# Rotary queries computed with channels on partitions: two heads per product, tables turned once, and one transpose group of the up stage issued nine products later

## The chip, the cores and the metric

The kernel runs on one NeuronCore of one Trainium2 chip. The metric is the device time of one execution in microseconds (us); the time of a kernel is the median of its runs. Five engines work side by side, each through its own queue in order: TensorE (PE, matrix products, with a separate row PEld for loading weights), VectorE (DVE), ScalarE (ACT), GpSimd (POOL) and SyncE (SP, which issues the DMAs). They wait for each other by semaphores. Products land in PSUM, which has eight banks of 128 x 512 floats.

## The reference, cut to what matters

One layer of a streaming encoder on 512 tokens of width 1024, in float32. The first sub-layer has three parallel token mixers (pooling, latent attention, spatial gating), merged by gates; the second is a gated MLP with a short convolution. The change is in the attention's rotary queries (and, for one group of transposes, at the start of the MLP):

```python
def _apply_rope(x, cos, sin):
    x1, x2 = jnp.split(x, 2, axis=-1)                 # 32 + 32 channels
    return jnp.concatenate([x1 * cos - x2 * sin, x2 * cos + x1 * sin], axis=-1)

q = jnp.einsum('bsr,rhd->bshd', _rms_norm(cq, g_q), w_uq)      # 8 heads, 128 + 64 channels
q_nope, q_rope = q[..., :128], q[..., 128:]
q_rope = _apply_rope(q_rope, cos[:, :, None, :], sin[:, :, None, :])
k_rope = _apply_rope(kr, cos, sin)                             # one rotary key for all heads
s = einsum('bqhd,bkhd->bhqk', q_nope, k_nope) + einsum('bqhd,bkd->bhqk', q_rope, k_rope)
p = softmax(mask(s * 192 ** -0.5)); o = einsum('bhqk,bkhd->bqhd', p, v)
```

cos and sin depend on the token and on one of 32 frequencies, not on the head.

## The kernel before

Nearly every product is made from float32 operands that are split in a rounded high part and a low remainder (`...h`, `...l`); a product is then three matmuls, high by low, low by high and high by high (`mm3`, lines 106 to 108; `mm_chunk`, lines 113, 114 and 116, which is 24 matmuls of 512 columns over the eight 128-row pieces of the contraction). The split is one ScalarE cast (line 92 or 120) and one VectorE subtraction (line 93 or 121).

The program begins with the latent stage: products with eight pieces of the normalised input leave 448 latent channels for each of four token tiles in four PSUM banks (`lat`), tokens on partitions. ScalarE squares them (`sq`), POOL makes the norms (`rr`), ScalarE scales them (`cn`, lines 601 and 602). TensorE meanwhile computes gate blocks: `gate(b, m)` is one `mm_chunk` of 24 matmuls into a bank `pg`, and a Tanh on ScalarE (line 404). Twelve transposes (line 619, `ptc`) turn the normalised latents to channels on partitions, giving `cT0`, `cT1` (queries) and `cT2` (keys and values); nine more (`ptk`) turn the rotary key.

Rotary queries before: `rotary_queries` multiplies each token tile's latents by all 512 rotary channels (24 matmuls for four tiles, bank `pq`, tokens on partitions), multiplies the result on VectorE by tables `cosQ` and `sinQ` with the frequencies along the free axis (lines 661), combines halves on POOL (lines 669 and 672), splits into high and low on ScalarE and VectorE (lines 679 and 680), and leaves tiles `qst` in which a head has 64 high and 64 low channels side by side. `rotary_transposes(h)` then turns a head's four token tiles with four TensorE transposes (line 690, `ptq`) and one copy to `qrT`. Heads 0 to 3 are turned before the head loop, head h + 4 in the loop of head h.

The head loop: `scores(h)` (banks `sc`), `attend(h - 1)` (`po`), `project(h + 1)` (`pqn`), one gate block, `transposes(h)` (`ptp`, the probabilities turned, split to `PTh`, `PTl`). `scores(h)` needs `qrT[h]`. The bank that a `sc`, `pg` or `po` gets is the one that another tile has just given up, so a reader on ScalarE or VectorE that is late holds up TensorE.

The up stage (first products of the MLP) starts on the first two token tiles (columns 0 to 255) while the last two are still being normalised: `up_early(ms, half)` computes one half of the columns of output blocks `pzu`. `turn(tp, jp)` transposes two token tiles of the second normalisation `xr` (four transposes, `pth`), and `second_modulation` makes `h2T` out of it. `turn(1, 0)` is the first group that needs the last token tile.

The order on each engine is set when the program is built, by a scheduler that places instructions by its own estimate of time; `tc.issue_after` fixes single orders by hand. On the chip each engine then takes its queue strictly in that order.

## Time and profile before

| | before |
|---|---|
| time, median of 3 runs | 960.9 us (960.22 to 961.87) |
| the profiled execution's own time | 961.97 us |
| its span, first to last instruction | 960.2 us |
| granted TensorE clock, mean | 0.998 |
| PE busy | 946.6 us, 99% of the span |
| DVE, ACT, POOL busy | 579.6, 380.7, 285.1 us |
| HBM read | 116.83 MB, 124 GB/s over the span |

A profile is one execution. In a row of the timeline the first number is the start in us from the span's beginning, the second the length of the row (with its fellows, where "x8" says that eight follow each other), then engine, line, operation, output<-inputs, sizes; in brackets stands how long the engine was idle before, and what it waited for. Instructions of one engine overlap: the next one starts before the one ahead has ended, so the step from start to start is less than the length. In a row of the windows each engine has its busy time and count in that stretch, and then stand the granted clock (1.00 is full) and the DMA's share and rate.

### The profile page before, as it was taken

The numbers are of one execution on the slowest core, as the hardware profiler recorded it, in microseconds if no ns is written. First come the engines' busy times: TensorE is split into PE (matmuls) and PEld (weight loads), VectorE is DVE, ScalarE is ACT, GpSimd is POOL, SyncE is SP. The second block draws the span as 40 slices with busy tenths as digits, with TensorE's granted clock in tenths as the row PEclk, the third lists the DMA queues.
The fourth block names the chain that finished last, engine by engine and source line by source line (L and its number), as shares of the span: only waits on it lengthen the run. The fifth ranks groups of instructions, "written<-read, shape, count | busy, mean of one in ns | idle before, by whom it ended". The sixth has DMA issues, their size and how long they took to land.

```text
span 960.2 us, 12180 instructions
## 1 busy us (share of the span) xinstructions
PE 946.6 (99%) x4591; PEld 800.6 (83%) x4591; DVE 579.6 (60%) x841; ACT 380.7 (40%) x622; POOL 285.1 (30%) x257
## 2 busy tenths in 40 slices
PE   7999999999999999999999999999999999999996
PEld 6988888888888888888888889988888888888885
DVE  6968556456686566477333489576565564733368
ACT  4575556543333322233332345554444444322121
POOL 3752110122350023202112713021111121756653
PEclk9999999999999999999999999999999999999999
DMA  9812122045435633554343450134334433333222
GB/s 343 297 56 84 63 61 82 24 134 155 150 100 204 199 123 89 172 195 148 114 127 110 146 184 23 48 128 119 123 112 135 128 113 106 123 104 104 88 88 88
DMA packets 46139, 119.72 MB, mean 125 GB/s; under 512 B 5504, under 2 KB 8960, under 8 KB 46080
## 3 DMA queue, kind: packets, MB, share of 16 engines
q1 hardware_dynamic: 45648, 118.39, 38.1%
q8 instruction: 36, 0.59, 0.2%
q10 hardware_dynamic: 432, 0.55, 0.2%
q14 instruction: 23, 0.19, 0.1%
HBM read 116.83 MB, written 2.10 MB: 124 GB/s over the span
## 4 chain that ended last, share of the span: by engine, by line
PE 90%; DVE 4%; POOL 2%; DMA 1%; ACT 1%; issue 1%; POOLq 0%; SPq 0%; DVEq 0%; ACTq 0%
PE pzu L113 7%; PE pzu L114 7%; PE pzu L116 7%; PE pg L113 4%; PE pg L114 4%; PE pg L116 4%; PE py L113 4%; PE py L114 4%; PE py L116 4%; PE pyd L1149 3%; PE pyd L1152 3%; PE pyd L1151 3%; PE lat L531 2%; PE pu L113 2%; PE pu L114 2%; PE pa L113 2%
## 5 line engine op out<-in xcount | busy, mean ns | idle before, releaser
L93 DVE TENSOR_TENSOR wupl<-wup,wuph 128x1024 fp32r<-128x1024 f32 x38 | 48.2, 1270 | 71.8 <-PE pzu L116 45.8
L1118 POOL TENSOR_TENSOR d<-d,gtfb 128x512 f32<-128x512 f32 x44 | 73.4, 1690 | 37.8 <-DMA d<-in_wdn 37.2
L1421 POOL TENSOR_TENSOR zc<-zc 128x512 f32<-128x512 f32 x22 | 29.6, 1347 | 173.5 <-ACT zc L1420 131.4
L1123 DVE TENSOR_TENSOR dl<-d,dh 128x1024 fp32r<-128x1024 f32 x18 | 29.3, 1627 | 55.0 <-PE pyd L1149 50.2
L92 ACT CAST wuph<-wup 128x1024 fp32r<-128x1024 f32 x38 | 39.9, 1051 | 47.1 <-PE pzu L114 47.1
L422 POOL TENSOR_TENSOR mg<-mg,th 128x512 f32<-128x512 f32 x16 | 31.3, 1959 | 86.5 <-DVE th L419 86.5
L93 DVE TENSOR_TENSOR wgl<-wg,wgh 128x1024 fp32r<-128x1024 f32 x22 | 29.0, 1320 | 42.5 <-PE pg L116 21.6
L92 ACT CAST wbh<-wb 128x1024 fp32r<-128x1024 f32 x24 | 25.3, 1054 | 74.0 <-PE py L114 55.3
L872 DVE SCALAR_TENSOR_TENSOR ada<-adar,cact,ada 128x512 f32<-128x512 f32 x56 | 49.1, 906 | 0.5 <-DMA adar<-in_ada 0.5
L787 POOL TENSOR_SCALAR pe<-pe,mx 128x128 f32<-128x128 f32 (+3 forms) x32 | 17.0, 537 | 94.0 <-DVE mx L786 47.9
L1122 ACT CAST dh<-d 128x1024 fp32r<-128x1024 f32 x18 | 19.0, 1054 | 62.5 <-PE pyd L1152 42.0
L1403 ACT ACTIVATE zc<-pzu,cols 128x512 f32<-128x512 f32 x44 | 34.2, 780 | 22.3 <-PE pzu L116 17.8
L93 DVE TENSOR_TENSOR wbl<-wb,wbh 128x1024 fp32r<-128x1024 f32 x24 | 30.3, 1262 | 14.9 <-ACT wbh L92 6.5
L1406 DVE SCALAR_TENSOR_TENSOR zc<-pzu,cols,zc 128x511 f32<-128x511 f32 x44 | 32.6, 743 | 4.0 <-ACT zc L1403 4.0
L92 ACT CAST wgh<-wg 128x1024 fp32r<-128x1024 f32 x22 | 23.2, 1054 | 26.6 <-PE pg L114 22.1
L1410 DVE SCALAR_TENSOR_TENSOR zc<-pzu,cols,zc 128x510 f32<-128x510 f32 x44 | 32.6, 745 | 0.8
L419 DVE SCALAR_TENSOR_TENSOR th<-th,py 128x512 f32<-128x512 f32 x16 | 11.0, 687 | 35.6 <-PE py L116 35.6
L1420 ACT ACTIVATE zc<-zc 128x512 f32<-128x512 f32 x22 | 13.9, 631 | 40.5 <-DVE zc L1410 40.4
L925 POOL TENSOR_TENSOR asum<-apad 128x527 f32<-128x527 f32 x8 | 12.3, 1543 | 54.6 <-ACT apad L920 28.0
L300 DVE SCALAR_TENSOR_TENSOR acc<-ada,cact,acc 128x256 f32<-128x256 f32 (+1 forms) x29 | 26.2, 903 | 1.0
L1097 POOL TENSOR_TENSOR oraw<-oraw,gttb 128x512 f32<-128x512 f32 x6 | 10.5, 1778 | 47.2 <-DMA oraw<-in_wo 47.2
L1118 POOL TENSOR_TENSOR o<-o,gttb 128x512 f32<-128x512 f32 x10 | 17.1, 1736 | 12.8 <-DMA o<-in_wo 10.0
(1478 smaller groups left out, 3095.8 us busy)
## 6 DMA issues: line engine op xcount, KB each, us to landing
wup<-in_wup SPq DMA_DIRECT2D x44, 512.0 KB, 3.6
adar<-in_ada SPq DMA_DIRECT2D x64, 256.0 KB, 3.9
wb<-in_wb SPq DMA_DIRECT2D x24, 512.0 KB, 3.6
wg<-in_wg SPq DMA_DIRECT2D x22, 512.0 KB, 3.6
d<-in_wdn SPq DMA_DIRECT2D x22, 512.0 KB, 3.5
ada<-in_ada1p SPq DMA_DIRECT2D x24, 256.0 KB, 5.1
wa<-in_wa SPq DMA_DIRECT2D x8, 512.0 KB, 3.6
wsg<-in_wsg SPq DMA_DIRECT2D x8, 512.0 KB, 3.5
```

The costliest lines, as they stand in the source:

```text
L92: nc.scalar.copy(out=hi[:, :n], in_=raw[:, :n])
L93: ins = nc.vector.tensor_tensor(out=lo[:, :n], in0=raw[:, :n], in1=f(hi[:, :n]), op=ALU.subtract)
L113: nc.tensor.matmul(o, wh[:, c], xl[k], start=k == 0, stop=False)
L114: nc.tensor.matmul(o, wh[:, c], xh[k], start=False, stop=False)
L116: nc.tensor.matmul(o, wl[:, c], xh[k], start=False, stop=k == KT - 1)
L422: nc.gpsimd.tensor_tensor(out=merged[m], in0=merged[m], in1=th, op=ALU.add)
L872: nc.vector.scalar_tensor_tensor(out=acc[n], in0=src, scalar=cact[:, k : k + 1], in1=acc[n], op0=ALU.mult, op1=ALU.add,)
L1118: nc.gpsimd.tensor_tensor(out=halves[n], in0=halves[n], in1=gt[n], op=ALU.mult)
L1403: nc.scalar.activation(t, pz, AF.Identity, bias=cols[:, cc + 3 : cc + 4], scale=cols[:, cc + 2 : cc + 3])
L1406: nc.vector.scalar_tensor_tensor(out=t[:, 1:512], in0=pz[:, 0:511], scalar=cols[:, cc + 1 : cc + 2], in1=t[:, 1:512], op0=ALU.mult, op1=AL ...
L1410: nc.vector.scalar_tensor_tensor(out=t[:, 2:512], in0=pz[:, 0:510], scalar=cols[:, cc : cc + 1], in1=t[:, 2:512], op0=ALU.mult, op1=ALU.add,)
L1421: nc.gpsimd.tensor_tensor(out=val, in0=val, in1=gate, op=ALU.mult)
```

## The change

Rotary queries are now made with channels on partitions and tokens along the free axis: `rotary(p)` computes the 128 rotary channels of heads 2p and 2p + 1 for all 512 tokens (six matmuls into `pq`), so nothing is left to transpose for a head. The tables must then have frequencies on partitions: ScalarE writes `cosRx` and `sinRx` with each table repeated four times with its sign and the scale (line 614 after), eight transposes turn them between gate blocks 2 and 3 (`ptr`, line 623), two ScalarE copies take them out of PSUM. A rotation is one VectorE product with the cosines and four on 32 partitions each, which read the partner channels' partitions for the sines (line 686), one POOL addition, and per head a ScalarE cast and a VectorE subtraction on 64 partitions. Since an odd head's high part is on the upper partitions, the low rotary key `krL` is now doubled instead of filled with zeros. The split of the rotary weights moves behind the key's transposes (`rotary_weights`, two casts of 512). In the loop, `rotary` follows `project` in heads 0, 2 and 4. In the up stage the first three of eight steps of block 5 are issued ahead of `turn(1, 0)`.

```diff
-        nc.scalar.activation(cosQ, cosT, AF.Copy, scale=SCALE)
-        nc.scalar.activation(sinQ, sinT, AF.Copy, scale=SCALE)
...
-    nc.gpsimd.tensor_tensor(out=krl, in0=ro, in1=kr[:, :, 0:64], op=ALU.subtract)
+    nc.gpsimd.tensor_tensor(out=krl[:, :, 0:64], in0=ro, in1=kr[:, :, 0:64], op=ALU.subtract)
+    nc.gpsimd.tensor_copy(out=krl[:, :, 64:128], in_=krl[:, :, 0:64])
...
-    for m in range(2, 4):
-        th0.append(gate(0, m))
+    turns = []
+    wide = []
+    for nm, src, signs in (("cosR", cosT, (1.0, 1.0)), ("sinR", sinT, (-1.0, 1.0))):
+        wide.append(act_t(nm + "x", F32))
+        for g, sign in enumerate(signs):
+            nc.scalar.activation(
+                wide[-1].rearrange("p (t a b f) -> p t a b f", a=2, b=2, f=32)[:, :, :, g, :],
+                src.rearrange("p t (a f) -> p t a f", a=1).broadcast_to([P, TT, 2, 32]),
+                AF.Copy, scale=sign * SCALE,
+            )
+    th0.append(gate(0, 2))
+    for nm, src in zip(("cosR", "sinR"), wide):
+        pt = ps("ptr")
+        for t in range(TT):
+            nc.tensor.transpose(pt[:, t * P : (t + 1) * P], src[:, t * P : (t + 1) * P], ident)
+        table = act_t(nm, F32)
+        nc.scalar.copy(out=table, in_=pt)
+        turns.append(table)
+    th0.append(gate(0, 3))
...
-    def rotary_queries():
-        wh, wl = wsplit(A["wqr"], D, "wqr")
-        for t in range(TT):
-            pq = ps("pq")
...
-    def rotary_transposes(h):
-        pt = ps("ptq")
...
+    def rotary_weights():
+        raw = load(A["wqr"], D, "wqr")
+        for k in range(2):
+            wh = act_t(f"wqr{k}h")
+            wl = act_t(f"wqr{k}l")
+            c = slice(k * 512, (k + 1) * 512)
+            nc.scalar.copy(out=wh, in_=raw[:, c])
+            nc.vector.tensor_tensor(out=wl, in0=raw[:, c], in1=f(wh), op=ALU.subtract)
+            wqr.append((wh, wl))
...
+    def rotary(p):
+        pq = ps("pq")
+        c = slice(p * P, (p + 1) * P)
+        for k in range(2):
+            wh, wl = wqr[k]
+            mm3(pq, wh[:, c], wl[:, c], cT_hi[k], cT_lo[k], k == 0, k == 1)
+        tA = pt_t("qtA")
+        tB = pt_t("qtB")
+        nc.vector.tensor_tensor(out=tA, in0=pq, in1=turns[0], op=ALU.mult)
+        for j in range(4):
+            o = slice(32 * j, 32 * j + 32)
+            i = slice(32 * (j ^ 1), 32 * (j ^ 1) + 32)
+            nc.vector.tensor_tensor(out=tB[o, :], in0=pq[i, :], in1=turns[1][o, :], op=ALU.mult)
+        nc.gpsimd.tensor_tensor(out=tA, in0=tA, in1=tB, op=ALU.add)
+        for h in range(2):
+            q = act_t(f"qrT{2 * p + h}")
+            hi = slice(64 * h, 64 * h + 64)
+            lo = slice(64 - 64 * h, 128 - 64 * h)
+            nc.scalar.copy(out=q[hi, :], in_=tA[hi, :])
+            nc.vector.tensor_tensor(out=q[lo, :], in0=tA[hi, :], in1=f(q[hi, :]), op=ALU.subtract)
+            qrT.append(q)
...
     attention_weights(0)
-    rotary_queries()
+    rotary_weights()
+    rotary(0)
     th0.append(gate(0, 4))
     project(0)
     values(0, (0, 1))
-    rotary_transposes(0)
     th0.append(gate(0, 5))
...
-        if h + 4 < H:
-            rotary_transposes(h + 4)
         if h + 1 < H:
             project(h + 1)
+        if h in (0, 2, 4):
+            rotary(h // 2 + 1)
...
-    with tc.issue_after(up_early((4,), 0)):
+    up_early((4,), 0)
+    with tc.issue_after(up_early((5,), 0, range(3))):
         ins = turn(1, 0)
     with tc.issue_after(ins):
-        up_early((5,), 0)
+        up_early((5,), 0, range(3, KT))
```

What the scheduler makes of it is not seen in the diff. First place: TensorE between gate blocks 2 and 3 (`wgh`, `wgl` are the gate weights' high and low parts, `hT` the input's pieces). Before:

```order
L116 MATMUL pg<-hT6h,wgl 128x512
L116 MATMUL pg<-hT7h,wgl 128x512
L113 MATMUL pg<-hT0l,wgh 128x512
L114 MATMUL pg<-hT0h,wgh 128x512
L113 MATMUL pg<-hT1l,wgh 128x512
```

And TensorE there after:

```order
L116 MATMUL pg<-hT6h,wgl 128x512
L116 MATMUL pg<-hT7h,wgl 128x512
L623 MATMUL ptr<-ident,cosRx 128x128 x4
L623 MATMUL ptr<-ident,sinRx 128x128 x4
L113 MATMUL pg<-hT0l,wgh 128x512
L114 MATMUL pg<-hT0h,wgh 128x512
```

The two table turns stand at the head of block 3, and what they read comes from ScalarE. The same stretch of ScalarE's queue, before:

```order
L601 ACTIVATE cn_748<-lat_191,rr 128x256
L92 CAST wqrh<-wqr 128x1024
L602 ACTIVATE cn_745<-lat_190,rr 128x128
L602 ACTIVATE cn_748<-lat_191,rr 128x128
L404 ACTIVATE th_790<-pg 128x512
L92 CAST wgh<-wg 128x1024
L404 ACTIVATE th_823<-pg 128x512
```

And after:

```order
L597 ACTIVATE cn_744<-lat_189,rr 128x256
L92 CAST wgh<-wg 128x1024
L598 ACTIVATE cn_741<-lat_188,rr 128x128
L598 ACTIVATE cn_744<-lat_189,rr 128x128
L614 ACTIVATE cosRx<-cosT 128x8x32 x2
L614 ACTIVATE sinRx<-sinT 128x8x32 x2
L400 ACTIVATE th_793<-pg 128x512
L625 COPY cosR<-ptr 128x512
L625 COPY sinR<-ptr 128x512
L92 CAST wvh<-wv 128x512
L400 ACTIVATE th_840<-pg 128x512
```

The split of gate 4's weights took the place of that of the rotary weights, and the four table copies stand behind the last `cn` and ahead of gate 2's Tanh.

Second place: the end of the key's transposes on TensorE (`pwm` is head 0's combined query weight). Before, the rotary product follows with weights that were split long ago:

```order
L635 MATMUL ptk<-ident,kr 128x128 x4
L638 MATMUL ptk<-ident,krf 128x128
L642 MATMUL ptk<-ident,krl 64x128 x4
L737 MATMUL pwm<-wqk_872 128x128 x2
L106 MATMUL pq<-wqrl,cT0h 128x512
L107 MATMUL pq<-wqrh,cT0l 128x512
```

TensorE there after:

```order
L649 MATMUL ptk<-ident,kr 128x128 x4
L652 MATMUL ptk<-ident,krf 128x128
L656 MATMUL ptk<-ident,krl 128x128 x4
L733 MATMUL pwm<-wqk_888 128x128 x2
L106 MATMUL pq<-cT0l,wqr0h 128x512
L113 MATMUL pg<-hT0l,wgh 128x512
L114 MATMUL pg<-hT0h,wgh 128x512
```

And ScalarE after, at that place (before, `wqk0h` is followed by `wvh`):

```order
L123 ACTIVATE cT2h<-ptc,cols 128x512
L650 CAST krT<-ptk 128x512
L642 ACTIVATE kF<-ptc,cols 128x128
L120 CAST wqk0h<-pwm 128x256
L668 CAST wqr0h<-wqr 128x512
L668 CAST wqr1h<-wqr 128x512
```

One matmul of the rotary product now stands ahead of gate block 4, and its weights are split right there. Third place: TensorE in the up stage, where block 4's products end (`upl` and `uph` are the up weights' parts). Before:

```order
L108 MATMUL pzu<-h2T7h,uph_5109 128x256
L1267 MATMUL pth<-ident,xr_5330 128x128
L1267 MATMUL pth<-ident,xr_5367 128x128
L1267 MATMUL pth<-ident,xr_5330 128x128
L1267 MATMUL pth<-ident,xr_5367 128x128
L106 MATMUL pzu<-h2T0l,uph_5336 128x256
```

And TensorE there after:

```order
L106 MATMUL pzu<-h2T0l,uph_5304 128x256
L107 MATMUL pzu<-h2T0h,upl_5306 128x256
L108 MATMUL pzu<-h2T0h,uph_5304 128x256
L106 MATMUL pzu<-h2T1l,uph_5304 128x256
L107 MATMUL pzu<-h2T1h,upl_5306 128x256
L108 MATMUL pzu<-h2T1h,uph_5304 128x256
L106 MATMUL pzu<-h2T2l,uph_5304 128x256
L107 MATMUL pzu<-h2T2h,upl_5306 128x256
L108 MATMUL pzu<-h2T2h,uph_5304 128x256
L1260 MATMUL pth<-ident,xr_5298 128x128 x2
L1260 MATMUL pth<-ident,xr_5335 128x128
L1260 MATMUL pth<-ident,xr_5298 128x128
```

Nine products of block 5 moved ahead of the group.

## The prediction

> **What bounds the kernel now.** I read the page first, then the windows, then each engine's timeline around the three places of the change.

> ```profile
> PE 946.6 (99%) x4591; PEld 800.6 (83%) x4591; DVE 579.6 (60%) x841; ACT 380.7 (40%) x622; POOL 285.1 (30%) x257
> ```

> ```profile
> 110.00:200.00 90.00, 90.00 (x501) 78.73 (x500) 46.98 (x127) 48.43 (x120) 14.95 (x29) 1.00 0.18 57
> 600.00:610.00 10.00, 9.25 (x78) 9.02 (x78) 4.14 (x10) 5.38 (x10) 1.67 (x3) 1.00 0.18 54
> ```

> TensorE is busy for 946.6 of 960.2 us (the first row), and its busy time fills the head loop's window to the last hundredth, at the full clock (the 1.00 behind the five engines). Of the windows around the change only 600 to 610 has a hole, of 0.75. So the time moves by two things alone: matmul time taken out of TensorE's queue, and every moment in which that queue waits. DVE (47 of 90 us in the head loop) and ACT matter only where TensorE's next instruction waits for them.

> **Transposes taken out.** 32 query transposes go (8 heads x 4), 8 table transposes come. The price is in a row of eight:

> ```profile
> 94.20 1.03 PE L690 MATMUL ptq<-ident,qst 128*128 128x128 f32 x8
> 95.07 0.61 PE L737 MATMUL pwm<-wqk 128*128 128x128 f32 x4
> ```

> Eight take 95.07 - 94.20 = 0.87 us, 0.109 each, so 24 fewer are -2.62. The rotary product keeps its 24 matmuls of 512 columns, only with the operands' roles exchanged. The low key's four transposes go from 64 to 128 columns in: the rows of both forms are equally long (0.60 for four, below), so nothing.

> **The table turns, between gates 2 and 3.** They wait for ACT, which is late there:

> ```profile
> 57.10 0.31 ACT L240 ACTIVATE sinQ<-sinT 128x128 f32<-128x128 f32 x1
> 57.31 0.30 ACT L239 ACTIVATE cosQ<-cosT 128x128 f32<-128x128 f32 x1
> 58.18 0.39 ACT L586 ACTIVATE sq<-lat 128x256 f32<-128x256 f32 x1 [0.58 <-PE lat L531]
> 64.46 1.16 ACT L92 CAST wqrh<-wqr 128x1024 fp32r<-128x1024 f32 x1
> 65.40 0.76 ACT L602 ACTIVATE cn<-lat,rr 128x128 f32<-128x128 f32 x2
> 65.91 0.73 ACT L404 ACTIVATE th<-pg 128x512 f32<-128x512 f32 x1
> 79.06 0.71 ACT L679 CAST qst<-qro 128x256 fp32r<-128x256 f32 x2
> 64.52 0.39 PE L113 MATMUL pg<-hT0l,wgh 128*128 128x512 f32 x1
> ```

> The removed `sinQ` and `cosQ` lay ahead of an idle 0.58 us of ACT, so taking them out brings ACT no earlier to the later rows. From 58.18 to 65.91 it works without a break, and after the change on work of the same sizes: gate 4's split takes the place of the rotary weights' (both a cast of 128x1024). So the first table copy starts at 65.91. No row shows this copy (256 elements per partition, written in runs of 32); nearest is the cast of 128x256 from SBUF, 0.71 for two, next start after 0.31. The cosine table is done at 65.91 + 0.71 = 66.62, the sine table at 65.91 + 3 x 0.31 + 0.40 = 67.24. TensorE has finished gate 2 at 64.52. It turns the cosines from 66.67 (0.05 for the semaphore, an estimate: further down `kF` starts at 73.73, 0.03 after `cT2l` has ended at 72.95 + 0.75), the sines from 67.29, and begins gate 3 at 67.73. With 0.87 of work it would be 65.39: **+2.34 of waiting**, and since TensorE takes its queue in order, gate 3 waits with the turns, though its weights are there. Bounds: with the step of `sinQ` (0.21, length 0.30) 1.95; with that of the `cn` copies of 128x256 (0.36, length 0.56) 2.65. I take the middle, since its size and source are the same.

> **The rotary weights' split, ahead of gate 4.** After gate 3 TensorE turns latents and key and comes to the first rotary matmul, which now waits for `wqr0h` at the end of an ACT chain:

> ```profile
> 68.15 0.27 PE L619 MATMUL ptc<-ident,cn 128*128 128x128 f32 x1
> 70.11 1.36 PE L619 MATMUL ptc<-ident,cn 128*128 128x128 f32 x11
> 71.31 0.60 PE L635 MATMUL ptk<-ident,kr 128*128 128x128 f32 x4
> 71.86 0.60 PE L642 MATMUL ptk<-ident,krl 128*64 128x128 f32 x4
> 72.66 0.48 PE L106 MATMUL pq<-wqrl,cT0h 128*128 128x512 f32 x1
> 72.22 0.69 ACT L123 ACTIVATE cT2h<-ptc,cols 128x512 fp32r<-128x512 f32 x1
> 72.95 0.75 DVE L124 SCALAR_TENSOR_TENSOR cT2l<-ptc,cols,cT2h 128x512 fp32r<-128x512 f32 x1
> 73.73 0.37 ACT L628 ACTIVATE kF<-ptc,cols 128x128 f32<-128x128 f32 x1 [0.34 <-DVE cT2l L124]
> 74.00 0.36 ACT L120 CAST wqk0h<-pwm 128x256 fp32r<-128x256 f32 x1
> 78.46 0.62 ACT L92 CAST wvh<-wv 128x512 fp32r<-128x512 f32 x1 [4.09 <-issue]
> ```

> Let T be the end of gate 3 (70.11 before, when it had begun at 64.52: less the one transpose 5.48 for 24 matmuls, 0.228 each; after 67.73 + 5.48 = 73.21). TensorE reaches the rotary product at T + 2.55 before, at T + 2.66 after (the transpose of 68.15, which stood inside the block, now stands behind it). On ACT `wqk0h` starts at T + 3.89, with that one transpose T + 4.00; its path (`cT2h`, DVE's `cT2l`, `kF`) is unchanged. `wqr0h` follows 0.26 later (0.36 less the overlap that rows show) and takes 0.62, the row of a 128x512 cast: done at T + 4.88, TensorE goes on at T + 4.93 = 78.14. **+2.27 of waiting**. Before, this split lay at 64.46, when nobody needed it. Bounds: a cast as short as the one of 128x256 (0.40) gives 2.05, one as long as a whole 128x1024 (1.16) 2.8; the row of the same size decides. Behind the waiting matmul stands gate 4, whose weights were split at 64.46: it could run and doesn't. The weights' buffer is free later too: on SP's queue the load of gate 5's weights, and behind it those of gate 6 and of head 1, move from 67 to about 79.4, when DVE has made `wqr1l`. Gate 5 comes at 87.7, 8 us later, so that is hidden. POOL loses a memset and gains a copy of the low key, in the 8.93 us that the row of its first rotary step shows as idle.

> **DVE, POOL and the head loop.** A pair of heads costs DVE five products from PSUM, POOL one addition of 128x512, ACT two casts, DVE two subtractions:

> ```profile
> 77.35 0.68 DVE L661 TENSOR_TENSOR qtA<-pq,cosQ 128x512 f32<-128x512 f32 x1
> 77.95 0.68 DVE L661 TENSOR_TENSOR qtB<-pq,sinQ 128x512 f32<-128x512 f32 x1
> 77.58 0.74 POOL L669 TENSOR_TENSOR qro<-qtA,qtB 128x256 f32<-128x256 f32 x1 [8.93 <-DVE qtB L661]
> 80.37 1.19 POOL L669 TENSOR_TENSOR qro<-qtA,qtB 128x256 f32<-128x256 f32 x1
> 102.45 0.39 PE L108 MATMUL pqn<-cT1h,wqk1h 128*128 128x512 f32 x1
> 103.51 0.69 DVE L754 SCALAR_TENSOR_TENSOR q1l<-pqn,q1h 128x512 fp32r<-128x512 f32 x1 [2.52 <-ACT q1h L753]
> 106.95 0.61 PE L737 MATMUL pwm<-wqk 128*128 128x128 f32 x4
> 107.25 1.15 DVE L121 TENSOR_TENSOR PTl<-ptp,PTh 128x512 fp32r<-128x512 f32 x2
> 109.32 0.40 PE L774 MATMUL sc<-cT2l,q1h 128*128 128x512 f32 x1
> ```

> A product is 0.60 from start to start; I price those on 32 partitions the same, since they have the same 512 elements per partition. The first pair: TensorE ends its product at 78.14 + 26 x 0.228 = 84.1 (gate 4 in between), DVE's five end at about 87.3, POOL's addition at 89.1, ACT's casts at 90.2, DVE's subtractions at 91. Behind the casts ACT holds gate 4's Tanh, `q0h` and `V00h`, behind the subtractions DVE holds `q0l` and `V00l`. The scores come after 3 + 12 + 24 + 6 more matmuls and `pwm`, at 94.6: 3.5 us of cover, and Tanh and `q0h` take 1.1 of it. The tight spot is in head 0: counted from the end P of the projection (102.84 before), `q1l` ends at P + 1.36, five products add 3.0, gate weights 1.14, `PTl` 0.6: P + 6.1. The last score group of head 1 needs the bank that `PTl` then gives up; TensorE is there after 14 gate matmuls (3.2), 10 transposes (1.1) and the earlier scores (109.32 - 106.95 = 2.4), at P + 6.5. So it fits, by 0.3 to 0.4. ACT has the two casts in its queue until POOL's addition is done, and behind them the splits of `PTh` and of head 2's weights and head 1's first exponential, which TensorE needs at P + 8.8 to 9.0; the addition is 2 x 0.74 = 1.5 alone, 2 x 1.19 = 2.4 beside a DVE subtraction. With 1.8 it holds by about 0.2, with 2.4 TensorE waits 0.5. I take **+0.1**, bounds 0 and 0.6. In heads 2 and 4 the projection or the whole gate block lies between, 2 us more cover.

> **The up stage.** The four transposes waited for the last row tile; nine products now go first:

> ```profile
> 602.24 0.27 PE L1267 MATMUL pth<-ident,xr 128*128 128x128 f32 x1
> 603.26 0.55 PE L1267 MATMUL pth<-ident,xr 128*128 128x128 f32 x3 [0.75 <-ACT xr L1254]
> 603.56 0.36 PE L106 MATMUL pzu<-h2T0l,uph 128*128 128x256 f32 x1
> 602.39 1.52 ACT L1254 ACTIVATE xr<-x,rs 128x512 f32<-128x512 f32 x2 [7.29 <-POOL rs L145]
> 605.37 0.41 DVE L1297 TENSOR_TENSOR h2T0l<-h2f,h2T0h 128x256 fp32r<-128x256 f32 x1
> 606.94 0.28 PE L106 MATMUL pzu<-h2T0l,uph 128*128 128x256 f32 x1
> ```

> The step 602.24 to 603.26 is 0.91 longer than a transpose. Nine products of 0.12 (603.56 to 606.94 holds 24 of them and four transposes) are 1.08, so the group starts at 603.32 and does not wait. Next late is `h2T0l`: 605.78 before, some 0.2 later after, while its reader comes at 606.0 instead of 606.94. It just meets. **-0.82**, bounds -0.5 and -0.91.

> **Sum.** -2.62 + 2.34 + 2.27 + 0.1 - 0.82 = +1.27. The profiled execution had a span of 960.2 and a time of 961.97, 1.1 above the median of 960.9; its span would be 961.5, its time 963.2, the median **962.2**. All lower ends together give +0.5, all upper ones +2.9: 961.4 to 963.8. With 0.2% (1.9 us), about what a measurement of this kernel can tell from no change, that is mostly no change.

> **Rivals.** First, the turns and weights are in time and only the savings count: 960.9 - 3.4 = 957.5, or 959.9 if one of the two waits is there. For it speaks that ACT is busy for only 40% of the span; against it, that both places lie in a stretch where ACT's chain is the later one, by rows. Second, slower: products that read one group of 32 partitions and write another are slow. No row shows one. If each took twice 0.68, a pair would hold DVE 2.7 longer, and in head 0 `PTl` would come 2.4 behind TensorE: 964.6. It decides from about 0.25 per product, where the sum passes 1.9. Third, the clock. The two new holes are each over 2 us:

> ```profile
> 952.00:954.00 2.00, 0.81 (x7) 0.60 (x6) 1.93 (x6) 0.00 (x0) 0.85 (x1) 1.00 0.48 186
> 956.00:958.00 2.00, 0.00 (x0) 0.00 (x0) 1.04 (x2) 0.51 (x1) 0.96 (x1) 0.72 0.24 93
> ```

> The last matmul ends at 952.8, and the mean 0.72 says that the clock halved at 956.9, 4.1 us later. A hole of 2.3 us, or of 0.91 at 602, is shorter. If it did, with 4.1 us at half speed, each would cost 2.0: 966.2. [...]

> **Chances.** Forecast 0.69 (a fifth of it beyond +1.9), one wait absent 0.07, both absent 0.05, slow products 0.13, clock 0.04, something unseen 0.02. Faster by over 0.2%: 0.06. Within: 0.55 + 0.07 = 0.62. Slower: 0.14 + 0.13 + 0.04 + 0.01 = 0.32. The range leaves out both-absent, part of one-absent and the clock: 960.3 to 964.6.

> **What would show it.** Right: PE idle about 2.1 before `ptr` cosRx and 0.2 before sinRx, released by ACT; 2.3 before the first `pq`, released by ACT's rotary weights; no wait at `pth`; no new wait in the head loop above 0.5. Wrong: `ptr` or `pq` without idle time, DVE's sine products longer than 0.7, a clock under 1.00 after the holes, or a wait of `sc` for `PTl`.

## The result and the profile after

The changed kernel takes 966.3 us (median of 4 runs, 965.77 to 966.79) where the kernel before takes 961.1 beside it: a ratio of 1.0053, interval 1.0041 to 1.0065. It is slower by some 5 us, outside the range of the prediction. The profiled execution took 966.0 us with a span of 964.3, 4.1 more than the 960.2 of before. First the line of the page on the engines, then windows of the changed kernel (columns as in the prediction: length, then busy time of PE, PEld, DVE, ACT, POOL, then the granted clock, the DMA share and GB/s).

```profile
PE 946.4 (98%) x4567; PEld 799.1 (83%) x4567; DVE 586.9 (61%) x850; ACT 380.8 (39%) x623; POOL 284.2 (29%) x253
```

```profile
64.97:68.38 3.41, 1.75 (x11) 1.47 (x12) 1.23 (x1) 3.41 (x10) 3.31 (x7) 1.00 0.42 96
75.21:78.62 3.41, 1.38 (x11) 1.15 (x10) 3.10 (x6) 3.00 (x7) 0.00 (x0) 1.00 0.63 206
78.62:82.04 3.42, 3.42 (x10) 2.64 (x9) 0.80 (x2) 0.00 (x0) 0.00 (x0) 0.50 0.41 126
82.04:85.45 3.41, 3.41 (x16) 2.80 (x16) 0.00 (x0) 1.05 (x1) 0.00 (x0) 1.00 0.07 28
600.00:610.00 10.00, 10.00 (x87) 10.00 (x86) 5.90 (x12) 2.62 (x5) 2.72 (x5) 1.00 0.18 54
```

TensorE issues 24 matmuls fewer (4567 against 4591), yet its busy time fell by 0.2 us only, and not by 2.6. The largest part of the difference is in the window from 78.62 on: for 3.42 us the clock is 0.50, and 10 matmuls fill a window that holds some 16 at the full clock. Ahead of it lie two stretches with TensorE partly idle (1.75 and 1.38 busy of 3.41). At 600 to 610 the hole of 0.75 us is gone. The timeline of TensorE at the two holes and in the second head:

```profile
63.70 0.39 PE L116 MATMUL pg<-hT7h,wgl 128*128 128x512 f32 x1
66.63 0.66 PE L623 MATMUL ptr<-ident,cosRx 128*128 128x128 f32 x4 [2.54 <-ACT cosRx L614]
67.24 0.65 PE L623 MATMUL ptr<-ident,sinRx 128*128 128x128 f32 x4
75.52 0.61 PE L733 MATMUL pwm<-wqk 128*128 128x128 f32 x4
78.15 0.50 PE L106 MATMUL pq<-cT0l,wqr0h 128*128 128x512 f32 x1 [2.03 <-ACT wqr0h L668]
79.21 0.63 PE L113 MATMUL pg<-hT1l,wgh 128*128 128x512 f32 x1
104.53 0.39 PE L108 MATMUL pqn<-cT1h,wqk1h 128*128 128x512 f32 x1
111.70 0.50 PE L770 MATMUL sc<-cT2l,q1h 128*128 128x512 f32 x1 [0.15 <-DVE PTl L121]
114.58 0.51 PE L106 MATMUL pqn<-cT0l,wqk2h 128*128 128x512 f32 x1 [0.25 <-ACT wqk2h L120]
```

Both holes are where the prediction had them, released by the ScalarE instructions that it named. From start to start, less what a matmul (0.227) or transpose (0.109) takes, they cost 2.7 (66.63 - 63.70) and 2.2 us. The matmul at 79.21 is the sign of the half clock: the steps from there to 82.04 are 0.427 instead of 0.227, 1.7 us in all. In the second head TensorE waits for `PTl`, `wqk2h` and an exponential (which holds a bank): its steps are 0.31, 0.41 and 0.25 us longer there than normal, and the first steps behind them another 0.2 together, 1.2 us in all. The row at 104.53 is the last matmul of the projection ahead of them; the text comes back to it. The engines behind these waits:

```profile
65.73 0.85 ACT L614 ACTIVATE cosRx<-cosT 128x256 f32<-128x256 f32 x2
66.34 0.85 ACT L614 ACTIVATE sinRx<-sinT 128x256 f32<-128x256 f32 x2
77.47 0.63 ACT L668 CAST wqr0h<-wqr 128x512 fp32r<-128x512 f32 x1
106.88 2.79 DVE L686 TENSOR_TENSOR qtB<-pq,sinR 32x512 f32<-32x512 f32 x4
109.70 1.22 DVE L93 TENSOR_TENSOR wgl<-wg,wgh 128x1024 fp32r<-128x1024 f32 x1
109.82 2.26 POOL L687 TENSOR_TENSOR qtA<-qtA,qtB 128x512 f32<-128x512 f32 x1 [5.61 <-DVE qtB L686]
112.11 1.26 ACT L692 CAST qrT<-qtA 64x512 fp32r<-64x512 f32 x2 [2.58 <-POOL qtA L687]
```

What waits in the second head has two candidates: DVE's queue (five products, then a weight subtraction ahead of `PTl`), or POOL's addition, behind which ACT's queue stands.

### The profile page after: what moved, and what is told of

Read it like the earlier page. It is cut to its first block, busy times and chain, and to the rows that moved or that the text cites. A ratio compares the mean times of both kernels' runs of the same rounds, so it can differ in the third digit from the quotient of the medians.

```text
span 964.3 us, 12139 instructions
## 1 busy us (share of the span) xinstructions
PE 946.4 (98%) x4567; PEld 799.1 (83%) x4567; DVE 586.9 (61%) x850; ACT 380.8 (39%) x623; POOL 284.2 (29%) x253
## 4 chain that ended last, share of the span: by engine, by line
PE 90%; DVE 1%; POOL 0%; issue 0%; ACT 0%; POOLq 0%
PE pzu L114 7%; PE pzu L113 7%; PE pzu L116 7%; PE py L113 5%; PE py L114 5%; PE py L116 5%; PE pg L113 4%; PE pg L114 4%; PE pg L116 4%; PE pyd L1144 3%; PE pyd L1145 3%; PE pyd L1142 3%; PE pu L113 2%; PE pu L114 2%; PE pa L113 2%; PE pu L987 2%
## 5 line engine op out<-in xcount | busy, mean ns | idle before, releaser
L92 ACT CAST wuph<-wup 128x1024 fp32r<-128x1024 f32 x38 | 39.9, 1050 | 46.2 <-PE pzu L114 46.2
L92 ACT CAST wbh<-wb 128x1024 fp32r<-128x1024 f32 x24 | 25.3, 1054 | 73.5 <-PE py L114 55.3
L92 ACT CAST wgh<-wg 128x1024 fp32r<-128x1024 f32 x22 | 23.3, 1060 | 29.8 <-PE pg L114 19.8
```

The source lines that it names most:

```text
L92: nc.scalar.copy(out=hi[:, :n], in_=raw[:, :n])
```

## The experiments

All times are medians, all ratios are to the kernel before, run on the same chip (960.6 to 961.0). The theories carry the same letters throughout: A, the holes cost their length, and the clock halves wherever TensorE is idle for most of one window of 3.41 us (the length of the half clock in the profile above); B, it takes both holes; C, a wait taken away comes back elsewhere. D, P and V come with the experiments that they belong to; V and P are about the second head, V with DVE's queue as the cause and P with POOL's addition.

**The turns behind gate 3** (the first hole taken away):

```diff
     th0.append(gate(0, 2))
+    th0.append(gate(0, 3))
     for nm, src in zip(("cosR", "sinR"), wide):
 ...
         turns.append(table)
-    th0.append(gate(0, 3))
```

> The turns of the two tables stand behind gate 3 instead of between gates 2 and 3; all else as in the changed kernel. Theory A (each hole of TensorE costs its own length, and the clock is halved whenever TensorE is idle for more than about half of one of the 3.41 us windows that the clock's edges keep to, so that the second hole alone can do it): the first hole (2.8 us in the changed kernel) is gone, the second stays at 2.0 to 2.3 us because ScalarE's conversion of the rotary weights stands behind that of pwm; time 966.3 - 2.8 = about 963.5, and the half clock is still there in executions where the second hole lies well inside a window. Theory B (it takes both holes, the clock remembers the first): the half clock is gone as well, 966.3 - 2.8 - 1.7 = 961.8. Theory C (the hole only hides a lateness of ScalarE, which comes back at the next place): the second hole grows by what the first loses, up to 5 us, and the time stays within 0.5 us of 966.3.

961.8 us (11 runs, 960.61 to 963.67), ratio 1.0013 (1.0004 to 1.0021). The hole of the profiled execution and its windows:

```profile
75.15 0.50 PE L106 MATMUL pq<-cT0l,wqr0h 128*128 128x512 f32 x1 [2.02 <-ACT wqr0h L668]
```

```profile
71.57:74.98 3.41, 1.56 (x15) 1.37 (x12) 3.12 (x5) 3.06 (x8) 0.00 (x0) 1.00 0.59 197
74.98:78.40 3.42, 3.25 (x14) 2.73 (x15) 1.36 (x3) 0.64 (x2) 0.00 (x0) 1.00 0.26 59
```

The first hole is gone and the second stays as long as it was (2.02 against 2.03), so C falls. The median is the number of B (961.8) and not that of A (963.5), but the single runs say more. In this execution no half clock follows (1.00 in both windows). TensorE was busy for 1.56 of the 3.41 us of the first window, which hold most of the hole, against 1.38 in the changed kernel; where these 3.41 us begin is the author's estimate, since the clock has no edge there. The 11 runs fall in two groups with nothing between 961.95 and 963.22: seven with a mean clock of 0.997 to 0.998, mean time 961.20, and four with 0.995 to 0.996, mean 963.43. One hole of 2.02 us is thus followed by the half clock in some executions and not in others. That it was so in those four is inferred from their clock and time, since the profile is of one of the seven.

**The rotary weights converted ahead of gate 2** (the second hole taken away):

```diff
+    rotary_weights()
     th0.append(gate(0, 2))
 ...
     attention_weights(0)
-    rotary_weights()
     rotary(0)
```

> The rotary weights are converted ahead of gate 2, so that the first matmul of the rotary queries finds them; the turns stay between gates 2 and 3. Theory A: the second hole (2.0 to 2.2 us) and the half clock that lay behind it (1.7 us) go, the first hole stays, perhaps longer, since two ScalarE conversions of 0.63 us now stand ahead of it or near it: 966.3 - 2.2 - 1.7 = 962.4, up to 1.2 us more if the conversions stand ahead of the copies of the tables; a half clock behind the first hole is possible where that lies inside one window. Theory B (both holes needed): no half clock, 962.4. Theory C (lateness comes back): within 0.5 us of 966.3.

964.19 us (6 runs, 962.23 to 965.02), ratio 1.0032 (1.0021 to 1.0044). Its timeline, then its windows:

```profile
66.14 0.66 PE L636 MATMUL ptr<-ident,cosRx 128*128 128x128 f32 x4 [2.72 <-ACT cosRx L614]
76.97 0.48 PE L106 MATMUL pq<-cT0l,wqr0h 128*128 128x512 f32 x1
```

```profile
63.40:66.81 3.41, 0.69 (x6) 0.48 (x5) 1.43 (x2) 3.41 (x10) 3.35 (x5) 1.00 0.22 77
66.81:70.23 3.42, 3.42 (x11) 2.84 (x12) 1.34 (x2) 2.37 (x5) 2.02 (x4) 0.50 0.74 192
```

The first rotary matmul no longer waits. The half clock is still there, now behind the first hole alone, whose 2.72 us lie wholly in the 3.41 us ahead of the clock's fall at 66.81. B falls. The time is above the 962.4 that A gave without a half clock; with it, 966.3 less the second hole's 2.2 is 964.1. By time, four runs are near 964.4 and two near 962.4, again 2 us apart.

**Both moved** (the two edits above together):

> Both edits: the turns behind gate 3, the rotary weights converted ahead of gate 2. Theories A and B alike: neither hole nor half clock, 966.3 - 2.8 - 2.2 - 1.7 = 959.6, which is 1.5 us under the kernel before: the removed transposes (2.6 us) and the up stage (0.9 us) less the waits in the first heads (about 1.1 us) and what is left of ScalarE's work in the stage. Theory C: 965 or more, with the same idle time of TensorE at other places between 60 and 90 us.

960.18 us (11 runs, 959.52 to 960.59), ratio 0.9991 (0.9982 to 1.0001); the clock is 1.00 from 52 to 196 and from 586 to 956 us in the profiled execution, the mean clocks are 0.997 to 0.999 in all, and the runs lie within 1.1 us. Against the changed kernel that is 6.1 us, close to the 6.7 expected. What is missing stands in the second head:

```profile
98.55 0.39 PE L108 MATMUL pqn<-cT1h,wqk1h 128*128 128x512 f32 x1
105.73 0.50 PE L771 MATMUL sc<-cT2l,q1h 128*128 128x512 f32 x1 [0.84 <-DVE PTl L121]
108.59 0.49 PE L106 MATMUL pqn<-cT0l,wqk2h 128*128 128x512 f32 x1 [0.23 <-ACT wqk2h L120]
100.91 2.79 DVE L687 TENSOR_TENSOR qtB<-pq,sinR 32x512 f32<-32x512 f32 x4
103.85 2.24 POOL L688 TENSOR_TENSOR qtA<-qtA,qtB 128x512 f32<-128x512 f32 x1 [7.04 <-PE sc L775]
```

The waits there have grown from 1.2 to 1.9 us (1.0, 0.4 and 0.3 over the normal steps, and 0.2 behind them). That looks like C, but the traces show another cause. From the last matmul of the projection, behind which DVE starts its products, to the scores that wait for `PTl` it is 7.18 us here (105.73 - 98.55) and 7.17 in the changed kernel (111.70 - 104.53): DVE's chain is as long as before. What changed is TensorE's cover. The scheduler places the projection inside a gate block, and 14 matmuls of that block stand behind it in the changed kernel, 10 here, 0.9 us less. The two single edits tell the causes apart: with the turns moved (first hole gone) 14 stand there and the waits are as in the changed kernel (TensorE busy for 19.63 us of 100 to 120, there 19.60); with the weights moved (first hole and half clock still there) 10 stand there and the waits are as here (18.94 in both). So the order made the wait, not the time won, and C falls here too.

**The holes filled with matmuls** whose result nothing uses, 10 in the first and 8 in the second:

```diff
         pt = ps("ptr")
+        for i in range(10 if nm == "cosR" else 0):
+            nc.tensor.matmul(pt, hT_hi[0][:, 0:P], hT_lo[0], start=True, stop=True)
 ...
         pq = ps("pq")
         c = slice(p * P, (p + 1) * P)
+        for i in range(8 if p == 0 else 0):
+            nc.tensor.matmul(pq, cT_hi[0][:, 0:P], cT_lo[0], start=True, stop=True)
```

> The changed kernel with matmuls that nothing uses (operands that have long been ready, 0.227 us each, 1.8 to 2.3 us in each of the two holes: 10 ahead of the first turn, 8 ahead of the first matmul of the rotary queries, written to the bank that the following products overwrite): the holes cost the same time, but TensorE works in them. Theory A, the clock answers to idle time in a window: no half clock anywhere between the first 20 us and the tail, so 966.3 - 1.7 = 964.6 (up to 0.5 more where the last filler ends behind the operand). [...]

964.84 us (5 runs, 964.28 to 965.51), ratio 1.0043 (1.0030 to 1.0056). The stretches of the two holes:

```profile
64.58:67.99 3.41, 3.12 (x18) 2.28 (x17) 1.23 (x1) 3.41 (x10) 3.35 (x7) 1.00 0.46 93
74.82:78.23 3.41, 3.41 (x22) 2.95 (x21) 3.10 (x6) 2.97 (x8) 0.00 (x0) 1.00 0.72 211
```

With TensorE at work in the holes (busy for 3.12 and 3.41 of 3.41 us) the clock stays at 1.00, though the real work is nearly as late as before: the first turn starts 2.94 us behind gate 2's last matmul (2.93 in the changed kernel), and gate 4 stands behind 1.9 us of fillers where it stood behind a wait of 2.2. So in this kernel the half clock goes with the idle time; a theory D, by which something else lowers it at that place or time, falls. The time fell by 1.5 where 1.7 was expected. That number is no clean price, since the scheduler moved more than was asked: the first real rotary matmul went into gate 4, the weight subtraction of gate 4 went ahead of the first products on DVE, and only 8 gate matmuls stand behind the second head's projection, where the waits grew by about 1.3.

**The changed kernel once more**, unedited:

> The changed kernel once more, to see which hole the half clock follows. Theory A with the windows of 3.413 us in any phase, and half clock wherever TensorE was busy for less than about 0.43 of one: counted over all phases from the trace of the changed kernel, the half clock follows the first hole alone in 53 of 100, the second alone in 38, both in 9, neither in 1; so all runs lie near 966.3 (965.5 to 967), none near 964, unlike the version with the second hole alone (46 of 100). Theory B (the second hole trips it because of the first): always behind the second hole, at 78.6 us.

966.23 us (5 runs, 965.82 to 966.68), ratio 1.0055 (1.0041 to 1.0069).

```profile
75.86:79.27 3.41, 1.38 (x8) 1.01 (x7) 3.10 (x6) 2.45 (x6) 0.00 (x0) 1.00 0.53 184
79.27:82.69 3.42, 3.42 (x10) 2.64 (x9) 0.19 (x1) 0.00 (x0) 0.00 (x0) 0.50 0.49 153
```

Again behind the second hole, which does not tell the theories apart by itself. But no run of this kernel lies near 964, as A has it: the two holes start 12.0 us apart, three and a half times 3.41 us, and by A's count, an estimate of the author's, the half clock then follows at least one of them in 99 of 100 cases.

**The edit of the up stage alone**, on the kernel before (the last part of the diff):

> The kernel before with the edit of the up stage alone (the second transpose group behind the first 9 matmuls of block 5 instead of behind block 4). Theory, as in the prediction: the idle place of 0.75 us at 602.5 us closes, -0.8 to -0.9: 960.9 - 0.8 = 960.1. Rival (the place is bound by ScalarE's and VectorE's h2 pieces and only moves): no change, 960.9.

960.06 us (11 runs, 959.57 to 961.13), ratio 0.9993 (0.9984 to 1.0002). The window of this kernel, then that of the kernel before:

```profile
590.00:612.00 22.00, 22.00 (x186) 21.88 (x186) 13.96 (x30) 11.29 (x21) 4.32 (x8) 1.00 0.08 25
```

```profile
590.00:612.00 22.00, 21.25 (x179) 21.02 (x178) 14.41 (x30) 11.72 (x23) 4.49 (x8) 1.00 0.09 25
```

The hole of 0.75 is closed. From the first product of the up stage to the end of the span it is 372.4 us before and 371.6 in this kernel, in the changed one and in the last version below: -0.8 each time. The medians alone couldn't tell it from nothing.

**The second pair's addition on DVE**, on the version with both edits:

```diff
-        nc.gpsimd.tensor_tensor(out=tA, in0=tA, in1=tB, op=ALU.add)
+        (nc.vector if p == 1 else nc.gpsimd).tensor_tensor(out=tA, in0=tA, in1=tB, op=ALU.add)
```

> As the version with both edits (960.2), and the addition of the second pair (2.24 us on GpSimd) done by VectorE in that one pair. Theory P (the waits of TensorE in the second head, 1.9 us in all, stand behind GpSimd's addition, as the prediction had it): they shrink to 0.5 or less, 960.2 - 1.5 = 958.7. Theory V (they stand behind VectorE, which does the five products of the second pair, 3.5 us, and a weight subtraction, 1.2 us, between the first head's probabilities and their low parts): VectorE gets 0.7 us more just there, the wait for PTl grows from 1.0 us or stays, only what follows behind ScalarE's conversions (0.65 us) can go: 959.8 to 960.8.

960.58 us (11 runs, 959.89 to 961.42), ratio 0.9999 (0.9990 to 1.0008).

```profile
106.42 0.66 DVE L688 TENSOR_TENSOR qtA<-qtA,qtB 128x512 f32<-128x512 f32 x1
107.11 1.26 ACT L693 CAST qrT<-qtA 64x512 fp32r<-64x512 f32 x2 [4.22 <-DVE qtA L688]
109.14 0.39 ACT L120 CAST wqk2h<-pwm 128x256 fp32r<-128x256 f32 x1
109.59 0.51 PE L106 MATMUL pqn<-cT0l,wqk2h 128*128 128x512 f32 x1 [0.98 <-ACT wqk2h L120]
```

The addition takes 0.66 instead of 2.24, but it stands behind DVE's queue and starts at 106.42, where POOL had started at 103.85. The wait for `PTl` is the same (0.84), the one for `wqk2h` grew from 0.23 to 0.98. So P falls for the wait for `PTl`, the larger one, which did not move. The wait for `wqk2h` does hang on the addition, whichever engine does it: ACT's casts of `qrT`, which stand ahead of `wqk2h`, start when it ends (107.11 here, 106.12 in the version before). A faster engine for that step is no cure, since the queue ahead of it is the delay.

**The second pair ahead of the head loop**, on the version with both edits:

```diff
+    rotary(1)
     values(0, (2, 3))
 ...
-        if h in (0, 2, 4):
+        if h in (2, 4):
             rotary(h // 2 + 1)
```

> As the version with both edits (960.2), and the second pair's rotary queries formed ahead of the head loop (behind gate 5), where VectorE is less loaded, instead of in the first turn of the loop. Theory V: the waits of the second head (1.9 us) go, no new one of over 0.5 us comes: 960.2 - 1.9 = 958.3, up to 959 if the products delay the first head's maxima. Theory P: GpSimd's addition now stands ahead of the first head's normalisations instead; 1 to 2 us of waiting moves into the first head, 959.5 to 960.5.

967.46 us (5 runs, 965.66 to 968.13), ratio 1.0069 (1.0057 to 1.0082), a clear miss by both theories.

```profile
100.75 0.80 PE L106 MATMUL pqn<-cT0l,wqk1h 128*128 128x512 f32 x1 [6.23 <-ACT wqk1h L120]
```

```profile
95.99:99.40 3.41, 0.00 (x0) 0.00 (x0) 3.30 (x10) 3.35 (x8) 0.00 (x0) 1.00 0.22 77
99.40:102.81 3.41, 2.06 (x5) 1.68 (x6) 1.80 (x7) 1.97 (x6) 2.07 (x4) 0.50 0.00 0
102.81:106.23 3.42, 3.42 (x10) 2.65 (x9) 0.00 (x0) 0.00 (x0) 0.00 (x0) 0.50 0.00 0
```

The products (3.5 us) and a weight subtraction (2.28 us here) now stand on DVE ahead of the first head's maxima; ACT holds that head's exponentials ahead of `wqk1h`; and the next instruction in TensorE's queue is the projection that needs `wqk1h`. It is idle for 6.23 us, and the clock is at half for 6.8 us from 99.40 on. The expectations had the products' length right and overlooked who stands behind them.

**The queues of the second head reordered**, on the version with both edits:

```diff
+        if h == 0:
+            transposes(h)
         if len(th0) < KT:
             th0.append(gate(0, len(th0)))
 ...
-        transposes(h)
+        if h:
+            transposes(h)
```

and `rotary(1)` ends with its addition, its two casts and two subtractions being called after `scores(1)`.

> As the version with both edits (960.2); in the first turn of the head loop the transposes are written ahead of gate 6, so that the low parts of the probabilities stand ahead of the weight subtraction of 1.2 us on VectorE; and the conversions of the second pair (two on ScalarE, two on VectorE) are written behind the second head's scores, so that ScalarE converts wqk2h ahead of them. Theory V (TensorE's waits of 1.9 us in the second head are waits behind VectorE's and then ScalarE's queue, not behind GpSimd as such): the wait for PTl (1.0 us) and that for wqk2h (0.4 us) go, 0.3 us at the release of a bank by the exponentials stay: 960.2 - 1.4 = 958.8 (958.3 to 959.5). Theory P (GpSimd's addition of 2.24 us sets it): no change, 960.2.

958.47 us (6 runs, 956.88 to 959.39), ratio 0.9972 (0.9960 to 0.9983), faster than both kernels. DVE, then ACT, then windows of the stretch:

```profile
100.89 1.16 DVE L121 TENSOR_TENSOR PTl<-ptp,PTh 128x512 fp32r<-128x512 f32 x2 [1.36 <-ACT PTh L120]
101.96 1.22 DVE L93 TENSOR_TENSOR wgl<-wg,wgh 128x1024 fp32r<-128x1024 f32 x1
102.02 0.37 ACT L120 CAST wqk2h<-pwm 128x256 fp32r<-128x256 f32 x1
102.28 1.26 ACT L701 CAST qrT<-qtA 64x512 fp32r<-64x512 f32 x2
```

```profile
80.00:100.00 20.00, 20.00 (x100) 16.79 (x99) 15.24 (x30) 12.51 (x25) 4.79 (x6) 1.00 0.26 76
100.00:120.00 20.00, 20.00 (x115) 17.65 (x114) 13.38 (x37) 12.63 (x34) 4.24 (x8) 1.00 0.25 74
```

`PTl` now stands ahead of the weight subtraction and `wqk2h` ahead of the casts of `qrT`, and no wait is left: TensorE is busy for all of 80 to 120. It took 1.7 us off the version with both edits, where 1.4 was expected. POOL's addition, no longer beside a DVE subtraction, took 1.29 instead of 2.24 us, and the pair's products on DVE started some 3 us earlier (`qtB` at 96.74 against 100.91, 1.0 of it from an earlier start of the program), so how much of the gain belongs to each of the two moves is not told apart.

## Why the prediction was wrong, point by point

**Transposes, -2.62: right.** The last version shows it free of waits. The rows are the last transposes of the input and the first matmul behind the head loop, of the kernel before and then of that version:

```profile
53.46 0.63 PE L493 MATMUL pt<-ident,x 128*128 128x128 f32 x4
...
196.15 0.48 PE L113 MATMUL pa<-hT0l,wah 128*128 128x512 f32 x1
```

```profile
51.91 0.64 PE L489 MATMUL pt<-ident,x 128*128 128x128 f32 x4
...
191.99 0.48 PE L113 MATMUL pa<-hT0l,wah 128*128 128x512 f32 x1
```

142.69 us before, 140.08 then: -2.61, with all of the change's matmuls and DVE products in between.

**The first hole, +2.34: right in place and cause, and nearly in size.** The sines and cosines were copied from 65.73 (forecast 65.91), in steps of 0.31 as forecast. A copy takes 0.55 instead of 0.40, so the turns began only 0.04 earlier than forecast; that two errors cancelled there is luck. Gate 2 ended 0.6 earlier than in the trace of before, as the last transposes of the input did (last section), and ACT's copies did not come earlier by as much, so the hole is longer: 2.7.

**The second hole, +2.27: right**, 2.2 in both traces of the changed kernel.

**The up stage, -0.82: right**, -0.80.

**The slow products: the rival falls.** Four products on 32 partitions take 2.79 us, 0.70 from start to start, 0.1 more than the 0.60 priced.

**The head loop, +0.1: the step was mis-sized, and its cause partly wrong.** The bounds were 0 to 0.6; the trace has 1.2, and 1.9 where the scheduler leaves 10 gate matmuls behind the projection instead of the 14 that the forecast counted. The forecast put the end of `PTl` at P + 6.1 and TensorE at P + 6.5, P being the end of the projection. TensorE came at P + 6.5, `PTl` at P + 6.8: each DVE step was 0.1 longer than priced, and the margin of 0.4 was gone. The other doubt, POOL's addition, was set at 1.8 and took 2.26. With 0.2 of margin on one side and 0.4 on the other, the term should have had the larger bounds, not the smaller.

**The clock, 0: here the prediction failed.** The step that failed is the argument against the rival that was given a chance of 0.04: "A hole of 2.3 us, or of 0.91 at 602, is shorter", namely than the 4.1 us after which the clock had halved in the tail. The 4.1 us were read as a length that idle time must reach. The runs show that length alone does not decide: in the changed kernel the first hole (TensorE idle for 2.54 us) has the clock at 1.00 behind it, and the second, shorter one (2.03) has it at 0.50; in the version with the weights moved it is at 0.50 behind 2.72 us, and in the profile of the version with the turns moved it stays at 1.00 behind 2.02. In the changed kernel the first hole lies across two stretches of 3.41 us, counted back from the clock's fall at 78.62, in which TensorE was busy for 2.54 and 1.75 us, and the second inside one, with 1.38. That the place decides is the author's reading of this, theory A; no run moved a hole by itself. With it agree the edges of the clock in the first trace of the changed kernel, 10.36, 78.62, 82.04 and 959.26 us, which are 20, 1 and 257 times 3.413 us apart. The price by arithmetic, 3.41 us at half speed, is 1.7; the two groups of runs without the first hole differ by 2.2. The prediction's own price of 2.0 for one was about right, and the changed kernel pays it once in both of its profiles, not twice. Among its nine runs one has a mean clock of 0.994, where the profiled ones have 0.996, and may have paid twice. That the rival's 966.2 lies next to the measured 966.3 is luck: it had two half clocks, and one half clock, a longer first hole and the head loop came instead.

**The sum.** -2.62 + 2.7 + 2.2 + 1.7 + 1.2 - 0.8 = +4.4 by the trace of the changed kernel. The first steps behind the two holes are 0.3 longer than normal (67.24 - 66.63 is 0.61 for four transposes that take 0.44, and the step behind the matmul at 78.15 is 0.34), which makes 4.7. The changed kernel's profile started 0.6 earlier (below), so its span should be 4.1 longer, and it is. On the medians, 966.3 against 961.1, some 0.5 stays open. Without the clock the forecast's terms as measured give 2.7 to 3.0, a time of 963.6 to 963.9, within the range. By this sum the one step, whether the clock stays up, took the time out of the range; the head loop brought it near the end.

## What to carry to other kernels

A hole in TensorE is to be priced with what follows it: in these profiles holes of 2.03 and 2.72 us had 3.4 us of half clock behind them and one of 6.23 had 6.8, while holes of 2.02 and 2.54 us had none, and the changed kernel, with two holes, took 965.8 to 966.8 us in all nine runs. When a step is moved, look at the order that the scheduler makes elsewhere: a place with a thin margin can lose it without any work of its own being touched. Write down who stands behind the moved work on every engine's queue, in particular short conversions for TensorE behind long elementwise work. Here the same savings became +5.2 us in one order of turns, conversions and products, and -2.6 in another.

## What the runs showed of the hardware

| version | stretch, us | TensorE busy, us | share | clock behind |
|---|---|---|---|---|
| second pair ahead of the loop | 95.99 to 99.40 | 0.00 | 0.00 | 0.50 |
| weights moved | 63.40 to 66.81 | 0.69 | 0.20 | 0.50 |
| changed kernel | 75.21 to 78.62 | 1.38 | 0.40 | 0.50 |
| changed kernel once more | 75.86 to 79.27 | 1.38 | 0.40 | 0.50 |
| turns moved | 71.57 to 74.98 (start estimated) | 1.56 | 0.46 | 1.00 |
| changed kernel | 64.97 to 68.38 | 1.75 | 0.51 | 1.00 |
| second pair ahead of the loop | 92.57 to 95.99 | 1.94 | 0.57 | 1.00 |
| changed kernel | 61.55 to 64.97 | 2.54 | 0.74 | 1.00 |

What exactly is counted no run shows. In the changed kernel the half clock lasted for 3.42 us, with TensorE busy in all of them. In the version with the second pair ahead of the loop it lasted longer: TensorE was busy for 2.06 of the 3.41 us from 99.40, the next 3.42 us were at 0.50 too, with TensorE busy in all of them, and from 106.23 the clock was 1.00.

At the start the rate of the matmuls changes as well. In the kernel before, TensorE was busy for the whole of 9.40 to 13.40 us, with 7 matmuls (of 128x232) in the 2 us ahead of 11.40 and 12 in the 2 us behind; in the changed kernel it is 7 and 12 around 10.36. The last transposes of the input start at 53.46 us in the kernel before and at 52.87 in the changed one, 0.59 apart where those two times are 1.04 apart. That the one follows from the other no run shows. The profiled execution of before, 1.1 us above its median, is the one with the later change.

POOL's addition of 128x512 took 1.29 us alone, in the version with the queues reordered, and takes 2.24 to 2.33 in the traces where it starts just behind a DVE subtraction. When it starts first, it keeps its 1.27 and the subtraction is the longer one, as in the version with the second pair ahead of the loop (the subtraction takes 1.22 when it does not come second):

```profile
93.98 1.27 POOL L688 TENSOR_TENSOR qtA<-qtA,qtB 128x512 f32<-128x512 f32 x1 [9.52 <-DVE qtB L687]
94.06 2.28 DVE L93 TENSOR_TENSOR wgl<-wg,wgh 128x1024 fp32r<-128x1024 f32 x1
```

So in these rows the one that comes second is about 1 us longer (2.26 in the changed kernel's second head against 1.29 for the addition, 2.28 against 1.22 for the subtraction).
